# A two-layer attention and RWKV-7 backbone: two plain pairs and no GpSimd in the MLPs, low-rank weights in halves

## The chip, the cores and the metric

The kernel runs on one core of one Trainium2 chip. The metric is the device time of one execution in microseconds; the lower the better. The engines are named as the profile names them: PE is TensorE, DVE is VectorE, ACT is ScalarE, POOL is GpSimd, and SP issues the DMAs.

## What is computed

A trunk of 256 context tokens and 512 latent tokens of width 1024 passes two layers. Layer 0 is windowed attention and an MLP over all 768 tokens, layer 1 is RWKV-7 time mixing in both directions and an MLP over the 512 latent tokens alone. Everything is float32.

```python
def sq_relu_mlp(h, w1, w2):
    return jnp.square(jax.nn.relu(h @ w1)) @ w2          # D_FF = 4 * 1024
...
def rwkv_features(h, mu, w_rkv, w0, w1, w2, a0, a1, a2, k_k, k_a):
    xr, xw, xk, xv, xa, xg = [h + xx * mu[m] for m in range(6)]
    r = heads(xr @ w_rkv[0])
    k = heads(xk @ w_rkv[1])
    v = heads(xv @ w_rkv[2])
    decay = tuple(
        heads(jnp.exp(-jnp.exp(-jax.nn.softplus(-(w0[d] + jnp.tanh(xw @ w1[d]) @ w2[d]).astype(F32)) - 0.5)))
        for d in range(2))
    a = heads(jax.nn.sigmoid((a0 + (xa @ a1) @ a2).astype(F32)))
...
    def gate(d):
        return (jax.nn.sigmoid(xg @ g1[d]) @ g2[d]).astype(F32)
```

## The kernel before

Features lie on the 128 partitions, tokens along the free axis; 1024 features are 8 blocks, called `f` or `k`. A float32 product is made of three matmuls (`mm3`, L366, L368 and L370): each operand is split into a high part, a rounded copy (mostly on ACT), and a low part, the remainder (a subtraction, on DVE or POOL); high by high, high by low and low by high are added up in PSUM.

**The MLPs** (`mlp`). The hidden width 4096 is 32 tiles `m` of 128 columns of W1. Tiles are taken in pairs. One pair is plain: `first_pair` (matmuls at L762) runs 8 feature blocks x 3 x 2 token halves x 2 tiles, 96 matmuls. Fifteen pairs go through `pair`, a scheme of Winograd's kind with 7 half-size products in place of 8: 7 x 4 x 3 = 84 matmuls. A token half has H = 384 columns in the MLP of layer 0 (MLP0 below) and 256 in that of layer 1 (MLP1). The price of the seven products are sums on the side of the weights (`wsum`, L811 to L814, for each pair), sums on the side of the operand (`block_sums`, L698 to L718, once for each MLP, over 4 blocks `k` and 4 sums `b`, each split into `mbh` and `mbl`), and sums of the products (`add` into `keep` and `mrelu`, L799). The square of the ReLU is split into `hid` and multiplied by W2 (`w2`, L841 on) in 8 blocks; its result is added to the trunk X (L664, L860). POOL takes part: a11-a21 (L814), the low parts of products 1, 5 and 6 (L789), half of the operand's last two sums (L711, L713, L716) and in MLP0 each second low part of W2 (L852).

**The features** of layer 1 come from products with full weights (r, k, v) and from low-rank maps: `low` makes the 64 or 128 inner columns, `lora2` and `gate` the second product, one block `f` at a time. A decay block (`decay`, L1145) is a product (L1099), a sigmoid on ACT into `sg` (L1154) whose 12 boundary columns POOL sets to zero (L1152), a scan on DVE into `cs` (L1159, L1161) and a store. The second maps' weights come through `side_weights` (L1028): one 128x1024 matrix in two transfers of 512 columns (L1036), each split on ACT (L338) or POOL (L340) in turn and on DVE (L341). Each matrix is asked for when its first block begins (`if f == 0`).

**What sets the order.** A scheduler with a model of the engines' times lays out one queue for each engine before the run; each engine then works through its own in order, and an instruction that waits holds all behind it. SP's queue of DMAs is one of them. Tiles come from rings of a fixed number of buffers, so a new tile waits until the last user of the old one is done.

```python
with self.behind_norm():
    self.block_sums(u2, H, bh, bl)
...
(eng or nc.vector).tensor_tensor(wl, raw, wh.bitcast(F32), ALU.subtract)
...
nc.gpsimd.memset(sg[:, :, 64 * d:64 * d + 1], 0.0)
```

Of the kernel before, what the change touches and what calls it, by code (L numbers as in the profile page):

```python
# [9 lines left out]
F32 = mybir.dt.float32  # L10
# [164 lines left out]
class K:  # L175
# [522 lines left out]
    def block_sums(self, u2, H, bh, bl):  # L698
# [8 lines left out]
        for b, i in ((4, 0), (3, 1), (5, 2), (6, 3)):  # L707
            for k in range(4):
                t = ts[k][i]
                if b == 5:  # L710
                    nc.gpsimd.tensor_tensor(t, ts[k][0], t, ALU.subtract)  # L711
                if b == 6:
                    nc.gpsimd.tensor_tensor(t, t, ts[k][0], ALU.subtract)  # L713
                act = nc.scalar.activation(bh[:, b, k], t, AF.Copy)
                eng = nc.gpsimd if b == 6 else nc.vector
                lo = eng.tensor_tensor(bl[:, b, k], t, bh[:, b, k].bitcast(F32), ALU.subtract)  # L716
                if b == 5:
                    self.sums_ins = (act.ins, lo.ins)  # L718

    def mlp(self, l, bc):  # L720
# [15 lines left out]
        self.normed_w(u2, Xk, bc, g2, self.ada[:, u0 + 3], l, n, bh, bl)  # L736
        parts = self.halves if l == 0 else lambda ps: [(ps[:, 0:S], slice(0, S))]
# [12 lines left out]
        def first_pair():  # L750
            banks, ws = [self.big("w1_ps") for _ in range(2)], []
            for j in range(2):
                raw = mp.tile([P, 1024], F32, tag="w1raw", bufs=NRW[l], name="w1raw")
                nc.sync.dma_start(raw, a["w1"][l, j])
                ws.append([self.wp.tile([P, 1024], F32R, tag=t, name=t) for t in ("whi", "wlo")])
                self.split(raw, *ws[j], eng=1)
            for k in range(NF):
                q = ((0, 6), (1, 2))[k // 4]
                for ps, (wh, wl) in zip(banks, ws):
                    for w, t, e in ((wh, bh, 0), (wh, bl, 1), (wl, bh, 2)):  # L760
                        for h in range(2):
                            nc.tensor.matmul(ps[:, 512 * h:512 * h + H], w[:, k * P:k * P + P], t[:, q[h], k % 4],  # L762
                                             start=(k == 0 and e == 0), stop=(k == NF - 1 and e == 2))
            with self.behind_norm():
                self.block_sums(u2, H, bh, bl)
            hid = hid_pair()
            for j, ps in enumerate(banks):
# [3 lines left out]
                nc.scalar.activation(hid[0][:, j], r, AF.Square)  # L771
                nc.vector.tensor_tensor(r, r, r, ALU.mult)
                nc.vector.tensor_tensor(hid[1][:, j], r, hid[0][:, j].bitcast(F32), ALU.subtract)
            return hid

        def pair(m, hid, j):
# [8 lines left out]
            def product(tag, raw, b, eng=None):  # L785
# [3 lines left out]
                (eng or nc.vector).tensor_tensor(wl, raw, wh.bitcast(F32), ALU.subtract)  # L789
# [16 lines left out]
            def square(i):  # L806
                nc.vector.scalar_tensor_tensor(c[i], c[i], 0.0, c[i], ALU.max, ALU.mult)  # L807
                nc.scalar.activation(hid[0][:, j + i], c[i], AF.Copy)
                nc.vector.tensor_tensor(hid[1][:, j + i], c[i], hid[0][:, j + i].bitcast(F32), ALU.subtract)  # L809

# [6 lines left out]
            add(c11, product("t", a12, 1, nc.gpsimd), p1)  # L817
# [13 lines left out]

        def w1(g):
            hid = first_pair() if g == 0 else hid_pair()
            for j in range(0, GF, 2):
                if g or j:
                    with self.behind_norm() if GF * g + j == 2 else ExitStack():
                        pair(GF * g + j, hid, j)
            hids[g] = hid

        def w2(g):  # L840
# [3 lines left out]
            for m in range(8):  # L844
# [119 lines left out]
    def rwkv_features(self, xs, scan):  # L964
# [131 lines left out]
        def lora2(parts, w, x, f):  # L1096
            for i in range(2):
                for o, sl in parts:
                    nc.tensor.matmul(o, w[i][:, f * P:f * P + P], x[:, sl], start=(i == 0), stop=(i == 1))  # L1099

        def low(w, m):
# [3 lines left out]
            for k in range(NF):  # L1105
# [881 lines left out]
```

## Time and profile before

| | |
|---|---|
| runs | 2232.52, 2230.0 and 2235.05 us, median 2232.52 |
| profiled execution | 2226.51 us, span of the trace 2224.5 us |
| mean granted TensorE clock | 0.939 |
| TensorE (PE) busy | 1999.1 us, 90% of the span |
| VectorE (DVE) | 1597.0 us, 72% |
| ScalarE (ACT) | 992.5 us, 45% |
| GpSimd (POOL) | 441.1 us, 20% |

In the trace MLP0's first matmul is at 464.19 us and its stage ends near 986; the features follow until about 1320, the scans and the readout until about 1848, and MLP1 from 1855.70 to the end. Times in the trace are from the start of the span. A row of the timeline has the start, the duration, the engine, the line, the operation, its output and inputs, and in brackets how long the engine was idle before it and what ended that. A merged row ("x6") has the duration of the whole. Neighbouring instructions of an engine overlap a little, so the distance of two starts is shorter than one duration. Granted clock 1.00 is the 2.4 GHz level, and about half of it in a stretch means the 1.2 GHz level.

### The profile page before, as it was taken

The numbers are of one execution on the slowest core, as the hardware profiler recorded it, in microseconds if no ns is written. First come the engines' busy times: TensorE is split into PE (matmuls) and PEld (weight loads), VectorE is DVE, ScalarE is ACT, GpSimd is POOL, SyncE is SP. The second block draws the span as 40 slices with busy tenths as digits, with TensorE's granted clock in tenths as the row PEclk, the third lists the DMA queues.
The fourth block names the chain that finished last, engine by engine and source line by source line (L and its number), as shares of the span: only waits on it lengthen the run. The fifth ranks groups of instructions, "written<-read, shape, count | busy, mean of one in ns | idle before, by whom it ended". The sixth has DMA issues, their size and how long they took to land. (4 is left out here: it accounts for less than half of the span.)

```text
span 2224.5 us, 42844 instructions
## 1 busy us (share of the span) xinstructions
PE 1999.1 (90%) x16616; PEld 1690.3 (76%) x16616; DVE 1597.0 (72%) x3263; ACT 992.5 (45%) x2026; POOL 441.1 (20%) x470
## 2 busy tenths in 40 slices
PE   5999999979999999988979797698759887999999
PEld 4876766868999999976856686586648656899897
DVE  4465565378777777679687575988898658988774
ACT  4355454253223322336554446567747445334331
POOL 0123232034222232210111101000000103323220
PEclk8999999979999999988989898798879897999999
DMA  8345461112222122134255344113211312333322
GB/s 292 106 123 155 133 221 59 57 52 74 72 65 71 63 72 65 53 119 167 86 188 220 117 138 154 52 33 106 87 54 50 133 49 72 109 100 100 104 82 81
DMA packets 125115, 229.81 MB, mean 103 GB/s; under 512 B 13937, under 2 KB 48497, under 8 KB 124529
## 3 DMA queue, kind: packets, MB, share of 16 engines
q1 hardware_dynamic: 124912, 227.08, 31.3%
q8 instruction: 131, 2.15, 0.4%
q14 instruction: 72, 0.58, 0.1%
HBM read 191.80 MB, written 32.60 MB: 101 GB/s over the span
## 5 line engine op out<-in xcount | busy, mean ns | idle before, releaser
L366 PE MATMUL w_ps<-hid,w2h 128*128 128x512 f32 (+1 forms) x768 | 231.1, 356 | 0.3
L368 PE MATMUL w_ps<-hid,w2h 128*128 128x512 f32 (+1 forms) x768 | 230.7, 354 | 0.4 <-DVE hid L809 0.4
L370 PE MATMUL w_ps<-hid,w2l 128*128 128x512 f32 (+1 forms) x768 | 230.6, 354 | 0.0
L850 ACT ACTIVATE w2h<-w2raw 128x256 fp32r<-128x256 f32 (+1 forms) x192 | 92.9, 487 | 287.0 <-PE w_ps L368 259.7
L664 DVE SCALAR_TENSOR_TENSOR X<-w_ps,ada,X 128x256 f32<-128x256 f32 (+1 forms) x256 | 145.2, 610 | 101.0 <-PE w_ps L370 100.6
L366 PE MATMUL w1p_ps<-mbh,whi 128*128 128x384 f32 x420 | 142.4, 341 | 6.2 <-ACT whi L788 4.8
L370 PE MATMUL w1p_ps<-mbh,wlo 128*128 128x384 f32 x420 | 142.8, 341 | 4.4 <-DVE wlo L789 3.0
L366 PEld LDWEIGHTS w_ps<-hid,w2h 128*128 128x128 f32 x768 | 129.6, 188 | 18.1 <-DVE X L860 1.1
L368 PE MATMUL w1p_ps<-mbl,whi 128*128 128x384 f32 x420 | 142.4, 339 | 0.0
L368 PEld LDWEIGHTS w_ps<-hid,w2h 128*128 128x128 f32 x768 | 126.1, 188 | 20.9 <-DVE hid L809 0.6
L370 PEld LDWEIGHTS w_ps<-hid,w2l 128*128 128x128 f32 x768 | 125.9, 188 | 20.8
L366 PE MATMUL w1p_ps<-mbh,swh 128*128 128x256 f32 x420 | 120.7, 288 | 15.5 <-ACT swh L788 9.4
L368 PE MATMUL w1p_ps<-mbl,swh 128*128 128x256 f32 x420 | 119.9, 286 | 0.3 <-DVE mbl L716 0.3
L370 PE MATMUL w1p_ps<-mbh,swl 128*128 128x256 f32 x420 | 118.7, 285 | 0.0
L789 POOL TENSOR_TENSOR swl<-w1raw,swh 128x512 fp32r<-128x512 f32 x45 | 69.9, 1556 | 197.1 <-ACT swh L788 115.4
L568 DVE CUSTOM_DVE_ANT_0 sm<-sc_ps,consts,vecs 128x256 f32<-128x256 f32 (+2 forms) x96 | 71.5, 760 | 38.4 <-PE sc_ps L566 17.9
L1447 PE MATMUL g_ps<-pad,bk 128*128 128x128 f32 x640 | 95.8, 300 | 3.3 <-ACT pad L1444 1.7
L366 PEld LDWEIGHTS w1p_ps<-mbh,swh 128*128 128x128 f32 x420 | 81.4, 194 | 19.0 <-ACT swh L788 9.6
L1447 PEld LDWEIGHTS g_ps<-pad,bk 128*128 128x128 f32 x640 | 83.4, 205 | 13.4 <-ACT pad L1444 7.2
L852 POOL TENSOR_TENSOR w2l<-w2raw,w2h 128x256 fp32r<-128x256 f32 x64 | 58.1, 908 | 178.8 <-ACT w2h L850 178.8
L341 DVE TENSOR_TENSOR wlo<-wraw,whi 128x1024 fp32r<-128x1024 f32 (+1 forms) x57 | 55.1, 983 | 52.7 <-ACT whi L338 32.9
L583 POOL TENSOR_SCALAR sm<-sm,sums 128x256 f32<-128x256 f32 (+2 forms) x96 | 63.6, 681 | 128.7 <-DVE sums L581 57.9
(424 smaller groups left out, 5629.5 us busy)
## 6 DMA issues: line engine op xcount, KB each, us to landing
ada_w<-ada_w SPq DMA_DIRECT2D x160, 256.0 KB, 3.5
w1raw<-w SPq DMA_DIRECT2D x64, 512.0 KB, 3.3
w2raw<-w SPq DMA_DIRECT2D x128, 128.0 KB, 2.1
w2raw<-w SPq DMA_DIRECT2D x64, 256.0 KB, 2.7
kt<-ada_w SPq DMA_DIRECT2D x32, 256.0 KB, 5.1
feat<-cs SPq DMA_DIRECT2D x16, 390.0 KB, 2.4
cs<-feat SPq DMA_DIRECT2D x24, 260.0 KB, 2.8
wraw<-wq SPq DMA_DIRECT2D x8, 512.0 KB, 3.8
```

The source lines that it names most:

```text
L341: nc.vector.tensor_tensor(lo, raw, hi.bitcast(F32), ALU.subtract)
L366: nc.tensor.matmul(o, wh, cut(xh, sl), start=start, stop=False)
L368: nc.tensor.matmul(o, wh, cut(xl, sl), start=False, stop=False)
L370: nc.tensor.matmul(o, wl, cut(xh, sl), start=False, stop=stop)
L568: nc.vector.tensor_tensor_reduce(sm[:, :nk], ps[:, :nk], self.c["band"][:, b0:b0 + nk], rs[:, h:h + 1], self.v["sink"][:, hd:hd + 1], ALU. ...
L583: nc.gpsimd.tensor_scalar(sms[h][:, :nk], sms[h][:, :nk], sums[:, h:h + 1], 1.0, ALU.mult, ALU.mult)
L664: self.nc.vector.scalar_tensor_tensor(self.X[:, m, sl], ps[:, sl], self.ada[:, u, m, s:s + 1], self.X[:, m, sl], ALU.mult, ALU.add)
L789: (eng or nc.vector).tensor_tensor(wl, raw, wh.bitcast(F32), ALU.subtract)
L850: nc.scalar.activation(wh, raw, AF.Copy)
L852: eng.tensor_tensor(wl, raw, wh.bitcast(F32), ALU.subtract)
L1447: nc.tensor.matmul(g[:, P * k:P * k + P], it.BK[:, d, b + k], pv[:, :, k], start=True, stop=True)
```

## The change

- In both MLPs two pairs are plain, tiles 0, 1 and tiles 2, 3 (`plain_weights`, `plain_pair`), and fourteen go through `pair`. The weights of tile 2 lie in the ring of W2's tiles. The operand's block sums are made while the second plain pair runs; the last four go into tiles of the `keep` ring and are split behind that pair.
- In the MLPs all that POOL did is done on DVE. The first pair's square is made in the way of the others (`square`).
- `side_weights` gives halves of 128x512 from a ring of two for each of the high and the low part. The first half of a matrix is asked for in block 5 of the one before it, the second half in block 1 of its own use.

```diff
-        for b, i in ((4, 0), (3, 1), (5, 2), (6, 3)):
+        for b, i in ((4, 0), (3, 1), (5, 2)):
             for k in range(4):
                 t = ts[k][i]
                 if b == 5:
-                    nc.gpsimd.tensor_tensor(t, ts[k][0], t, ALU.subtract)
...
+                    nc.vector.tensor_tensor(t, ts[k][0], t, ALU.subtract)
+                self.sums_ins = self.block_split(b, k, t, bh, bl)
+        for k in range(4):
+            nc.vector.tensor_tensor(t4[k], ts[k][3], ts[k][0], ALU.subtract)
+
+    def block_split(self, b, k, t, bh, bl):
+        act = self.nc.scalar.activation(bh[:, b, k], t, AF.Copy)
+        lo = self.nc.vector.tensor_tensor(bl[:, b, k], t, bh[:, b, k].bitcast(F32), ALU.subtract)
+        return act.ins, lo.ins
...
+        def plain_weights(m, own):
+
+            raw = mp.tile([P, 1024], F32, tag="w1raw", bufs=NRW[l], name="w1raw")
+            nc.sync.dma_start(raw, a["w1"][l, m])
+            w = 1024 if own else P * GF
+            ws = []
+            for c in range(0, 1024, w):
+                if own:
+                    ws.append([self.wp.tile([P, w], F32R, tag=t, name=t) for t in ("whi", "wlo")])
+                else:
+                    ws.append([mp.tile([P, w], F32R, tag=t, bufs=5, name=t) for t in ("w2h", "w2l")])
+                self.split(raw[:, c:c + w], *ws[-1], eng=1)
+            return [(h[:, c:c + P], l_[:, c:c + P]) for h, l_ in ws for c in range(0, w, P)]
+
+        def plain_pair(ws, turns):
+
+            banks = [self.big("w1_ps") for _ in range(2)]
+            for i, k in [(i, k) for k in range(NF) for i in range(2)] if turns else itertools.product(range(2), range(NF)):
                 q = ((0, 6), (1, 2))[k // 4]
...
+        def square(c, hid, j):
+            nc.vector.scalar_tensor_tensor(c, c, 0.0, c, ALU.max, ALU.mult)
+            nc.scalar.activation(hid[0][:, j], c, AF.Copy)
+            nc.vector.tensor_tensor(hid[1][:, j], c, hid[0][:, j].bitcast(F32), ALU.subtract)
...
-                (eng or nc.vector).tensor_tensor(wl, raw, wh.bitcast(F32), ALU.subtract)
+                nc.vector.tensor_tensor(wl, raw, wh.bitcast(F32), ALU.subtract)
...
-            nc.gpsimd.tensor_tensor(a21, a11, a21, ALU.subtract)
+            nc.vector.tensor_tensor(a21, a11, a21, ALU.subtract)
...
         def w1(g):
-            hid = first_pair() if g == 0 else hid_pair()
+            if g == 0:
+                rs = plain_pair([plain_weights(0, True), plain_weights(1, True)], True)
+                with self.behind_norm():
+                    ws.extend([plain_weights(2, False), plain_weights(3, True)])
+                    self.block_sums(u2, t4, H, bh, bl)
+            hid = hid_pair()
...
+                elif m == 2:
+                    rs = plain_pair(ws, False)
+                    for i in range(2):
+                        square(rs[i], hid, j + i)
+                    for k in range(4):
+                        self.sums_ins = self.block_split(6, k, t4[k], bh, bl)
...
-                    eng = nc.gpsimd if l == 0 and m % 2 else nc.vector
-                    eng.tensor_tensor(wl, raw, wh.bitcast(F32), ALU.subtract)
+                    nc.vector.tensor_tensor(wl, raw, wh.bitcast(F32), ALU.subtract)
...
         def side_weights(src):
...
+            halves = {}
+
+            def part(f):
+
+                i = f // 4
+                if i not in halves:
+                    halves[i] = [rp.tile([P, 512], F32R, tag=t, bufs=2, name=t) for t in ("swh", "swl")]
+                    raw = tmp(512, "swr")
+                    nc.sync.dma_start(raw, src[:, 512 * i:512 * i + 512])
+                    self.split(raw, *halves[i])
+                return [t[:, f % 4 * P:f % 4 * P + P] for t in halves[i]]
+
+            part(0)
+            return part
...
         def decay(d, f):
-            if f == 0:
-                w2[d] = side_weights(a["lw2"][d])
+            if f == 1:
+                w2[d](4)
+            elif f == 5:
+                w2[d + 1] = side_weights(a["la2"] if d else a["lw2"][1])
```

`low`, `keys` and `gate` are changed in the manner of `decay`.

The order of two queues shows what moved. First DVE at the start of MLP1, before: the operand's block sums are split at L716 (`mbl<-nu,mbh`), the weight sums are made at L811 to L813 and split at L789 (`swl`), a product is added at L799.

```order
2495 L812 TENSOR_TENSOR wsum<-wsum,w1raw 128x512
2496 L716 TENSOR_TENSOR mbl<-nu,mbh 128x256 x6
2497 L813 TENSOR_TENSOR wsum<-w1raw,wsum 128x512
2498 L716 TENSOR_TENSOR mbl<-nu,mbh 128x256 x2
2499 L799 TENSOR_TENSOR mrelu<-w1p_ps,keep 128x256
2500 L716 TENSOR_TENSOR mbl<-nu,mbh 128x256 x2
2501 L789 TENSOR_TENSOR swl<-wsum,swh 128x512 x3
```

And DVE at the same place in the changed kernel (L718 splits the operand's sums, L819 to L822 make the weight sums, L802 splits them, L785 and L787 are the square and its remainder `hid`, L875 is the low part of W2):

```order
2616 L718 TENSOR_TENSOR mbl<-keep,mbh 128x256
2617 L820 TENSOR_TENSOR wsum<-wsum,w1raw 128x512
2618 L822 TENSOR_TENSOR w1raw<-w1raw 128x512
2619 L718 TENSOR_TENSOR mbl<-keep,mbh 128x256 x3
2620 L875 TENSOR_TENSOR w2l<-w2raw,w2h 128x512 x2
2621 L787 TENSOR_TENSOR hid_19564<-mrelu,hid_19563 128x512 x2
2622 L821 TENSOR_TENSOR wsum<-w1raw,wsum 128x512
2623 L787 TENSOR_TENSOR hid_19564<-mrelu,hid_19563 128x512
2624 L812 TENSOR_TENSOR mrelu<-w1p_ps,keep 128x256
2625 L785 SCALAR_TENSOR_TENSOR mrelu<-mrelu 128x512
2626 L875 TENSOR_TENSOR w2l<-w2raw,w2h 128x512
2627 L802 TENSOR_TENSOR swl<-wsum,swh 128x512 x3
```

The split of the weight sums has moved behind all block sums, behind the first low parts of W2 and behind the hidden tiles of the second plain pair; a11-a21 (L822) has come into the queue from POOL.

Second, POOL among the decays, before (`swh<-swr` splits a half of a low-rank matrix, `whi<-wraw` weights of r and k):

```order
158 L1152 MEMSET sg 128x12
159 L340 TENSOR_SCALAR swh<-swr 128x512
160 L340 TENSOR_SCALAR whi<-wraw 128x1024
161 L1152 MEMSET sg 128x12
162 L340 TENSOR_SCALAR whi<-wraw_11127 128x512
163 L1152 MEMSET sg 128x12 x5
164 L340 TENSOR_SCALAR whi<-wraw_11340 128x512
165 L1152 MEMSET sg 128x12 x2
166 L340 TENSOR_SCALAR swh<-swr 128x512
167 L1152 MEMSET sg 128x12 x7
```

And in the changed kernel:

```order
52 L1188 MEMSET sg 128x12 x2
53 L340 TENSOR_SCALAR whi<-wraw 128x1024
54 L340 TENSOR_SCALAR swh<-swr 128x512
55 L1188 MEMSET sg 128x12 x2
56 L340 TENSOR_SCALAR whi<-wraw_11129 128x512
57 L1188 MEMSET sg 128x12 x2
58 L340 TENSOR_SCALAR swh<-swr 128x512
59 L340 TENSOR_SCALAR whi<-wraw 128x1024
60 L1188 MEMSET sg 128x12 x3
61 L340 TENSOR_SCALAR whi<-wraw_11340 128x512
62 L1188 MEMSET sg 128x12 x7
```

The split for the second direction stood behind nine memsets and ahead of seven; it now stands behind six and ahead of ten.

## Rows read from the trace of the kernel before

**Rows 1.** Windows (bounds, length, busy us and count by engine, PEclk, DMA): MLP0, features.
```profile
484.00:500.00 16.00, 8.92 (x32) 7.77 (x32) 13.24 (x15) 8.59 (x19) 16.00 (x11) 0.70 0.09 33
500.00:510.00 10.00, 8.36 (x45) 7.50 (x44) 9.84 (x10) 4.90 (x9) 10.00 (x8) 0.97 0.09 28
510.00:520.00 10.00, 8.11 (x46) 7.11 (x44) 9.97 (x12) 2.09 (x4) 5.44 (x4) 1.00 0.30 92
...
600.00:700.00 100.00, 100.00 (x577) 93.32 (x576) 74.11 (x123) 29.47 (x57) 28.76 (x26) 1.00 0.21 69
...
1100.00:1150.00 50.00, 39.36 (x188) 29.57 (x187) 40.28 (x39) 26.64 (x46) 8.92 (x18) 0.90 0.45 163
```

**Rows 2.** Windows of MLP1; order of the columns PE, PEld, DVE, ACT, POOL, as above.
```profile
1873.70:1883.00 9.30, 0.00 (x0) 0.00 (x0) 9.30 (x13) 3.31 (x10) 8.15 (x10) 0.63 0.00 0
1883.00:1887.00 4.00, 3.88 (x19) 3.77 (x20) 3.84 (x8) 4.00 (x10) 2.30 (x2) 0.59 0.42 135
...
1892.00:1897.00 5.00, 0.67 (x3) 0.67 (x4) 5.00 (x8) 2.15 (x5) 0.98 (x1) 0.61 0.38 126
1897.00:1902.00 5.00, 5.00 (x23) 4.45 (x23) 5.00 (x10) 1.21 (x3) 2.16 (x1) 0.70 0.26 88
1902.00:1907.00 5.00, 5.00 (x44) 5.00 (x43) 5.00 (x7) 2.40 (x5) 4.33 (x3) 1.00 0.27 103
...
2000.00:2100.00 100.00, 99.95 (x639) 90.84 (x638) 77.75 (x121) 39.50 (x68) 28.46 (x20) 1.00 0.30 98
```

**Rows 3.** Timeline of TensorE at the start of MLP0.
```profile
482.12 0.51 PE L762 MATMUL w_ps<-mbl,whi 128*128 128x384 f32 x2
...
483.51 0.34 PE L366 MATMUL w1p_ps<-mbh,whi 128*128 128x384 f32 x1
...
485.94 0.44 PE L370 MATMUL w1p_ps<-mbh,wlo 128*128 128x384 f32 x1 [1.45 <-DVE wlo L789]
...
492.74 0.69 PE L366 MATMUL w1p_ps<-mbh,whi 128*128 128x384 f32 x1 [4.77 <-ACT whi L788]
```

**Rows 4.** Timeline of TensorE at the start of MLP1.
```profile
1883.12 0.58 PE L366 MATMUL w1p_ps<-mbh,swh 128*128 128x256 f32 x1 [9.43 <-ACT swh L788]
...
1896.33 0.58 PE L366 MATMUL w1p_ps<-mbh,swh 128*128 128x256 f32 x1 [4.57 <-DVE keep L799]
```

**Rows 5.** Timeline of DVE at the start of MLP1.
```profile
1876.02 5.25 DVE L716 TENSOR_TENSOR mbl<-nu,mbh 128x256 fp32r<-128x256 f32 x6
...
1882.33 0.75 DVE L716 TENSOR_TENSOR mbl<-nu,mbh 128x256 fp32r<-128x256 f32 x2
```

**Rows 6.** Groups of L789 by form: durations in ns (min/median/max), first and last start.
```profile
L789 POOL TENSOR_TENSOR wlo<-w1raw,whi x45: 1283/1300/2009, 493.0 to 942.6; 128x512 fp32r<-128x512 f32 x45
L789 DVE TENSOR_TENSOR wlo<-wsum,whi x45: 673/681/1494, 494.9 to 930.1; 128x512 fp32r<-128x512 f32 x45
...
L789 DVE TENSOR_TENSOR wlo<-w1raw,whi x15: 678/1368/1767, 485.2 to 917.9; 128x512 fp32r<-128x512 f32 x15
```

**Rows 7.** The page's costliest groups: MLP0's update of X (busy, mean ns, idle).
```profile
L664 DVE SCALAR_TENSOR_TENSOR X<-w_ps,ada,X 128x256 f32<-128x256 f32 (+1 forms) x256 | 145.2, 610 | 101.0 <-PE w_ps L370 100.6
```

**Rows 8.** Timeline of all engines at the second direction's decays.
```profile
1124.86 0.86 SPq L1036 DMA_DIRECT2D swr<-lw  x2
...
1128.54 2.84 POOL L340 TENSOR_SCALAR swh<-swr 128x512 fp32r<-128x512 f32 x1 [5.19 <-DMA swr<-lw]
...
1131.43 0.80 PE L1099 MATMUL wl_ps<-tw,swh 128*128 128x512 f32 x1 [6.95 <-POOL sg L1152]
...
1134.54 11.91 DVE L1161 TENSOR_TENSOR_SCAN cs<-pm,sg 128x780 f32<-128x780 f32 x7 [1.42 <-ACT sg L1154]
...
1142.20 0.50 PE L366 MATMUL r_ps<-mxh,whi 128*128 128x512 f32 x1 [0.70 <-ACT sg L1154]
```

**Rows 9.** Timeline of TensorE at the gate.
```profile
1260.45 0.80 PE L366 MATMUL g_ps<-tw,swh 128*128 128x512 f32 x1 [4.29 <-ACT gt L1253]
```

**Rows 10.** Timeline of TensorE in the scan stage.
```profile
1658.04 2.19 PE L1522 MATMUL mg<-mt,gm 32*32 32x32 f32 x74 [19.37 <-DVE mt L1512]
```

More of the change, by code (lines that the diff above doesn't have):

```diff
@@ L736, in mlp @@
         self.normed_w(u2, Xk, bc, g2, self.ada[:, u0 + 3], l, n, bh, bl)
+        t4 = [mp.tile([P, H], F32, tag="keep", bufs=4, name="keep") for _ in range(4)]
         parts = self.halves if l == 0 else lambda ps: [(ps[:, 0:S], slice(0, S))]
@@ L748, in block @@
             return [w[:, 512 * h:512 * h + 512] for w in turn["w"]]
[L750 to L757, printed above, removed]
-                q = ((0, 6), (1, 2))[k // 4]
[L759 to L767, printed above, removed]
+        def plain_weights(m, own):
[10 more added lines that the diff above has]
+            return [(h[:, c:c + P], l_[:, c:c + P]) for h, l_ in ws for c in range(0, w, P)]
@@ new lines, in plain_pair @@
+        def plain_pair(ws, turns):
+            banks = [self.big("w1_ps") for _ in range(2)]
+            for i, k in [(i, k) for k in range(NF) for i in range(2)] if turns else itertools.product(range(2), range(NF)):
+                q = ((0, 6), (1, 2))[k // 4]
+                wh, wl = ws[i][k]
+                for w, t, e in ((wh, bh, 0), (wh, bl, 1), (wl, bh, 2)):
+                    for h in range(2):
+                        nc.tensor.matmul(banks[i][:, 512 * h:512 * h + H], w, t[:, q[h], k % 4],
+                                         start=(k == 0 and e == 0), stop=(k == NF - 1 and e == 2))
+            rs = []
+            for ps in banks:
@@ L822, in pair @@
             add(c12, p3, w)
-            square(0)
-            z = add(keep(), product("t", a21, 5, nc.gpsimd), q)
+            square(c[0], hid, j)
+            z = add(keep(), product("t", a21, 5), q)
             add(c22, p5, z)
-            add(c21, product("o", a22, 6, nc.gpsimd), z)
-            square(1)
+            add(c21, product("o", a22, 6), z)
+            square(c[1], hid, j + 1)
         def hid_pair():
             return [mp.tile([P, GF, n], F32R, tag=f"hid{i}", bufs=2, name=f"hid{i}") for i in range(2)]
+        ws = []
         def w1(g):
-            hid = first_pair() if g == 0 else hid_pair()
-            for j in range(0, GF, 2):
-                if g or j:
-                    with self.behind_norm() if GF * g + j == 2 else ExitStack():
-                        pair(GF * g + j, hid, j)
+            if g == 0:
[4 more added lines that the diff above has]
+            hid = hid_pair()
+            for j in range(0, GF, 2):
+                m = GF * g + j
+                if m == 0:
+                    for i in range(2):
+                        square(rs[i], hid, i)
+                elif m == 2:
+                    rs = plain_pair(ws, False)
+                    for i in range(2):
+                        square(rs[i], hid, j + i)
+                    for k in range(4):
+                        self.sums_ins = self.block_split(6, k, t4[k], bh, bl)
+                else:
+                    pair(m, hid, j)
             hids[g] = hid
@@ L1120, in low_decay @@
             th = tmp(T, "th")
-            for o, sl in (yield from low(w_lo, 1)):
+            for o, sl in (yield from low(w_lo, 1, lambda: w2.update(la1=side_weights(a["la1"])))):
                 nc.scalar.activation(th[:, sl], o, AF.Tanh)
@@ L1133, in low_rate @@
         def low_rate():
-            for o, sl in (yield from low(side_weights(a["la1"]), 4)):
+            for o, sl in (yield from low(w2["la1"], 4, lambda: w2.update({0: side_weights(a["lw2"][0])}))):
                 nc.scalar.activation(AH[0:64, sl], o[0:64], AF.Copy)
```

58 lines of the change are left out of this document (23 added, 35 removed).

## The prediction

> **What bounds the kernel now.** I read the windows first, then the timeline of TensorE around each window in which it is not full, then the groups by form for prices. In the middle of the MLPs TensorE is the bound: full at clock 1.00 for 100 us, with DVE at 74.11 and POOL at 28.76 beside it [rows 1]; MLP1 has the same, 99.95 with DVE at 77.75 [rows 2]. What the change does to DVE there is free as long as DVE stays under TensorE's pace. The time lies at three starts. In 484 to 500 TensorE does 32 matmuls at clock 0.70 [rows 1]. In 1873.7 to 1883 it does nothing, in 1892 to 1897 three matmuls, and then 23 where the next 5 us hold 44 [rows 2]. Among the features, 1100 to 1150 holds 50.00-39.36 = 10.64 us of idle TensorE [rows 1].
>
> The reader should see in the MLP starts a busy DVE beside an idle TensorE: 9.30 of 9.30 us [rows 2]. TensorE names DVE wlo and ACT whi in MLP0 [rows 3], ACT swh and DVE keep in MLP1 [rows 4]; these come late because the weight sums that they split stand in DVE's queue among the operand's block sums, and because both are stretched: six 128x256 remainders take 5.25 us, 0.87 each, while two a little later take 0.75, a pitch of 0.33 for a duration of 0.41 [rows 5].
>
> **Part 1, the second plain pair.** It adds 96-84 = 12 matmuls to each MLP. In MLP0 eight of this form take 483.51-482.12 = 1.39 us [rows 3], 0.174 each: +2.1 us. In MLP1 44 take 5.00 us [rows 2], 0.114 each: +1.4 us. Against this stands cover. A plain pair needs neither block sums nor weight sums: 96 x 0.174 = 16.7 us of TensorE in MLP0 and 96 x 0.114 = 10.9 in MLP1, in which DVE makes the sums.
>
> MLP0: 32 matmuls at 0.174 are 5.6 us, so 484 to 500 loses 10.4, of which 1.45 and 4.77 are the two waits [rows 3] and the rest is half clock and small gaps; the next two stretches idle 1.64 and 1.89 [rows 1]. Together 13.9; less 2.1, it can bring 11.8 at most. I walked DVE's new queue with the short prices (0.33, 0.47 and 0.60 us for 256, 384 and 512 columns; the first is a row's pitch [rows 5], the others are estimates from it and from the 673 of a 512 [rows 6], in proportion). The second pair's weights are split by about 486.5, a gap that the two products standing ahead in TensorE's queue fill; the last sum is split at about 501, when TensorE has just ended the second pair, and w2 of the first pair follows. I take **-11**, ends -12 and -4 (one wait comes back, with its half clock, 7).
>
> MLP1, lost by the same count: 9.3, 5.00 - 3 x 0.114 = 4.7, 5.00 - 23 x 0.114 = 2.4, and 4.00 - 19 x 0.114 = 1.8 [rows 2], together 18.2; less 1.4, 16.8 at most. But here the cover is short. TensorE has 10.9 us behind 1873.7, to about 1884.6. DVE has in that time 16 plain remainders, four L711 and four L714 at 0.33, the second pair's 1024 columns, three squares, four weight sums and two w2l, which by the short prices ends with two remainders of hid at about 1887. So w2 waits some 2.4 us, a keep in the pair behind it perhaps 1, and the clock may fall once more, as it did for 2.4 in 1897 to 1902. 16.8 less 5.8 is 11, and 13.4 if the clock holds. I take **-13**, ends -17 and -6.
>
> **Part 2, no POOL in the MLPs.** Per pair four 128x512 operations go to DVE, and in MLP0 four w2l of 256 columns. POOL takes 1283 ns at least for a wlo, DVE 673 for the same form [rows 6]. The cost at the starts is in the walks above. In the steady part, 45 POOL wlo from 493.0 to 942.6, three in a pair [rows 6], put a pair at some 31 us; DVE gets 4 x 0.60 + 4 x 0.33 = 3.7 us, 12% of it. What DVE has now is 74% [rows 1], but part of that is stretch: wlo<-w1raw has the form of wlo<-wsum and a median of 1368 against 681, though its minimum is 678 [rows 6]. By short prices DVE's own work in a pair is three sums and four remainders at 0.60, seven adds at 0.47, four steps of the square at 0.87, four w2l at 0.33 and 16 updates of X at about 0.5 (mean 610, with its other form, [rows 7]): some 20.5 us, 66%; with the addition 78%. With the stretch kept it is 74 + 12 = 86%. Both stay under TensorE's 100, so I take **0**: the 3.7 us are hidden behind TensorE, and without that cover they would cost 3.7 in each of 14 pairs.
>
> The Trainium skill ("SBUF — State Buffer", section "Who interferes with whom") says that a DVE instruction with two SBUF inputs and a POOL instruction that reads SBUF exclude each other, each for the whole of the other's time. By that rule the stretch goes with POOL and the 78% would hold, with the sum as it is; the doubled median agrees.
>
> **Part 3, the halves.** The chain at the second decay is plain: SP asks for swr<-lw at 1124.86, POOL stands with the split until 1128.54+2.84 = 1131.38, the memsets of sg queued behind it come only then, and TensorE waits 6.95 us for one [rows 8]. Then the eight decays run as fast as DVE's scans, seven in 11.91 us, until r_ps starts at 1142.20 [rows 8]. In the new order the second matrix is asked for and split within the first direction. Undone: 6.95, and 1 to 2 of what follows, as less stands behind the scans at the end. At the gate the first product behind a wait waits 4.29 [rows 9] for ACT's gt; with the halves split earlier the gate starts a v block sooner, and I count 3 of it. That is 11.5, and I take **-10**, because the 14 transfers and splits stay what they are and each now stands amid decays, where a split that waits for its DMA (up to 3.68 us, from SP's issue to POOL's start, [rows 8]) holds the sg behind it. Ends -15 and -2.
>
> **Part 4, what moves along.** The order of the scan stage changes a little too. TensorE has a wait of 19.37 us for DVE there [rows 10], so a reordering can give or take some. No row says which way: 0, ends -5 and +10.
>
> **Sum.** -11 - 13 + 0 - 10 + 0 = -34 against the profiled 2226.51. The median of the runs is 2232.52, 6.0 above; 2232.5 - 34 = **2198.5**.
>
> **Rivals.**
> A, the feature waits only move: the halves queue on SP, which is in order, behind the stores of cs, and the sg behind the splits. For it: the swr of before were issued late, not slow to land [rows 8]. Against it: in POOL's new queue two memsets or more stand between a split and the next. Gain 2 instead of 10: 2206.5. Chance 0.17.
>
> B, the second pair does not cover the sums: DVE is full through all of 1873.7 to 1907 [rows 2], and a sum that is late holds the products behind it. Then -6 in MLP1 and -8 in MLP0: 2208.5. Chance 0.13.
>
> C, DVE becomes the bound (the slower side). Place: every pair of both MLPs; remainders, sums, adds, squares and w2l share one queue in order. Price: where a wait of s us is left in each of 28 pairs, 28 s; the change turns slower where s passes 34/28 = 1.2. What decides is whether DVE's work in a pair passes TensorE's 31 us, or comes late in bursts. For it: MLP1 has 77.75 already [rows 2], and if 1368 [rows 6] is what such an operation costs with POOL silent too, four more make 74 + 18 + 4 = 96% and each burst is late. Against it: 678 and 681. With s = 1.7, +48: 2246. Chance 0.06.
>
> D, the scan stage loses one more wait like [rows 10], +19: 2217.5. Chance 0.07.
>
> E, more than forecast: both starts whole, -12 and -17, the features -15, the scan -3: 2185.5. Chance 0.10.
>
> The forecast itself: 0.47.
>
> **How the numbers follow.** The range runs from E to just above D, 2185 to 2220, and leaves out C, half of E and D together with A or B, some 0.17. A difference of 0.2%, 4.5 us, is about what a measurement of this kernel can tell from none. Faster by more than that: all but C and the joint upper tail, 0.88. Within it 0.05, slower 0.07.
>
> **What would show it.** Right: no wait of TensorE above 3 us in either MLP start; wlo<-w1raw on DVE at a median near 681; DVE at 76 to 80 in a full 100 us of MLP0 with TensorE at 100; no wait of TensorE for a POOL sg above 2 us, and r_ps some 8 us nearer to the start of the features. Wrong: TensorE under 98 in the steady part with DVE named (C), a wait of some 6 us for sg at another decay (A), w2 of MLP1 waiting over 6 us for hid (B), a longer way from the features to MLP1 (D).

## The result and the profile after

The changed kernel takes 2198.33 us, median of 4 runs (2191.91 to 2204.5), against 2231.26 (2229.87 to 2235.05) before: ratio 0.9849, 95% interval 0.9818 to 0.9881, 33 us faster. Forecast were 2198.5. The total came out; where it came from did not, as the experiments show. Two of the medians below, 2227.49 for the halves only and 2199.89 for gbc behind, count slow runs of 2331 and 4718 us and of 6409 us; without these they are 2226.09 and 2198.34.

The profiled execution takes 2196.83 us, span 2195.0, mean clock 0.943. PE is busy 1988.8 us (91%), DVE 1601.3 (73%), ACT 991.9 (45%), POOL 169.9 (8%, before 20%).

The windows that answer to [rows 1], start of MLP0 and its middle (length, then PE, PEld, DVE, ACT, POOL busy with counts, clock, DMA):

```profile
489.00:505.00 16.00, 16.00 (x94) 16.00 (x93) 16.00 (x30) 10.37 (x20) 0.00 (x0) 1.00 0.12 37
505.00:515.00 10.00, 10.00 (x59) 9.45 (x58) 9.71 (x18) 5.48 (x11) 0.00 (x0) 1.00 0.32 105
...
600.00:700.00 100.00, 100.00 (x576) 93.23 (x575) 80.17 (x148) 30.45 (x58) 0.00 (x0) 1.00 0.22 69
```

TensorE is full at once behind the first pair, at clock 1.00, where it did 32 matmuls in 16 us. In the middle nothing has changed for it: 576 matmuls in 100 us against 577, with DVE at 80.17 in place of 74.11.

What answers to [rows 2] and [rows 4], windows of MLP1 and the only waits of TensorE that the trace names between its first pair and the end:

```profile
1871.00:1876.00 5.00, 4.65 (x39) 4.33 (x37) 5.00 (x12) 4.13 (x9) 0.00 (x0) 1.00 0.00 0
1876.00:1881.00 5.00, 4.15 (x19) 3.45 (x20) 5.00 (x10) 3.45 (x7) 0.00 (x0) 1.00 0.62 210
```

```profile
1876.85 0.50 PE L368 MATMUL w_ps<-hid,w2h 128*128 128x512 f32 x1 [1.19 <-DVE hid L787]
1888.35 0.39 PE L366 MATMUL w1p_ps<-mbh,swh 128*128 128x256 f32 x1 [0.20 <-DVE keep L812]
```

The waits of 9.43 and 4.57 are gone; the one for hid that was expected at 2.4 is 1.19, and the clock doesn't fall. The whole of MLP1, before and after:

```profile
1855.70:2224.50 368.80, 347.55 (x2124) 312.60 (x2124) 286.49 (x438) 141.68 (x250) 101.24 (x72) 0.97 0.29 94
```

```profile
1846.60:2195.00 348.40, 342.13 (x2136) 309.46 (x2136) 275.53 (x494) 141.10 (x246) 0.00 (x0) 0.99 0.31 97
```

DVE does 56 instructions more in 11 us less, so its rows before were stretched. The groups by form that answer to [rows 6] say it outright (min/median/max in ns):

```profile
L802 DVE TENSOR_TENSOR wlo<-w1raw,whi x56: 678/683/692, 498.8 to 928.4; 128x512 fp32r<-128x512 f32 x56
```

In the features the wait of 6.95 for sg [rows 8] is gone and the one of 4.29 for gt [rows 9] is 0.51; in their place stand one for the remainder of a half (`swl`) and longer ones for `mxl`, the low part of the mixed input that k is made from:

```profile
1025.72 1.01 PE L368 MATMUL k_ps<-mxl,whi 128*128 128x512 f32 x2 [3.22 <-DVE mxl L1102]
...
1128.36 0.79 PE L1128 MATMUL wl_ps<-tw,swl 128*128 128x512 f32 x1 [1.73 <-DVE swl L341]
...
1133.53 0.76 PE L366 MATMUL r_ps<-mxh,whi 128*128 128x512 f32 x1 [0.58 <-ACT sg L1190]
...
1245.77 0.50 PE L366 MATMUL g_ps<-tw,swh 128*128 128x512 f32 x1 [0.51 <-ACT gt L1294]
```

So 6.95 + 4.29 = 11.2 us of waits went down to 0.5, but over all the features TensorE's idle time fell by 3.1 us only (363.43 - 320.53 = 42.9 before, 357.65 - 317.87 = 39.8 after). Its waits for mxl in the products of k went from 0.9 to 5.1 us together. `r_ps`, the first product behind the decays, starts 154.7 us behind the last update of X in MLP0 where it was 156.0: 1.3 us nearer, and 8 were forecast as a sign of being right.

Stage lengths tell more than totals here. Each number below is worked out from starts in one profiled execution: of MLP0's first matmul, of its last update of X, of the last gt, of MLP1's first matmul, and the end of the span. In the kernel before the last gt starts at 1349.66, so the features end there and not near 1320 as said above.

| kernel | to MLP0 | MLP0 | features | scan | MLP1 |
|---|---|---|---|---|---|
| before | 464.2 | 522.0 | 363.5 | 506.0 | 368.8 |
| changed | 469.1 | 509.7 | 357.7 | 510.1 | 348.4 |
| changed, again | 464.8 | 509.9 | 358.3 | 513.4 | 348.5 |
| halves only | 472.7 | 522.1 | 361.0 | 510.0 | 366.5 |
| both MLP parts | 463.9 | 510.6 | 362.2 | 504.6 | 349.4 |
| both MLP parts, again | 469.1 | 510.0 | 361.7 | 507.5 | 349.2 |
| no POOL only | 468.8 | 514.6 | 361.3 | 505.6 | 356.0 |
| plain pair only | 469.7 | 517.0 | 363.7 | 506.7 | 361.2 |
| low part twice | 474.6 | 511.0 | 354.9 | 513.6 | 353.3 |
| gate as before | 466.8 | 510.7 | 362.1 | 507.7 | 349.2 |
| decays as before | 467.8 | 509.8 | 358.1 | 513.9 | 349.3 |
| gbc behind | 470.3 | 510.4 | 355.8 | 514.7 | 348.5 |
| lanes first | 469.1 | 510.2 | 356.5 | 502.0 | 349.4 |

The first column is the attention, whose code no kernel here touches: 464 to 475, with 4.3 and 5.2 us between two executions of one kernel. A good part of what single totals differ by lies there; in the two kernels that were profiled twice the other columns repeat within 0.6 us in the MLPs and the features and within 3.3 us in the scan.

### The profile page after: what moved, and what is told of

Same layout as the page of the kernel before. It is cut to its first block, busy times and chain, and to the rows that moved or that the text cites. A ratio compares the mean times of both kernels' runs of the same rounds, so it can differ in the third digit from the quotient of the medians.

```text
span 2195.0 us, 42674 instructions
## 1 busy us (share of the span) xinstructions
PE 1988.8 (91%) x16640; PEld 1687.8 (77%) x16640; DVE 1601.3 (73%) x3443; ACT 991.9 (45%) x2022; POOL 169.9 (8%) x262
## 5 line engine op out<-in xcount | busy, mean ns | idle before, releaser
L664 DVE SCALAR_TENSOR_TENSOR X<-w_ps,ada,X 128x256 f32<-128x256 f32 (+1 forms) x256 | 145.8, 611 | 74.3 <-PE w_ps L370 73.8
L366 PEld LDWEIGHTS w_ps<-hid,w2h 128*128 128x128 f32 x768 | 130.6, 188 | 16.7 <-ACT w2h L874 0.7
L368 PE MATMUL w1p_ps<-mbl,whi 128*128 128x384 f32 x392 | 131.9, 337 | 0.0
L370 PE MATMUL w1p_ps<-mbh,wlo 128*128 128x384 f32 x392 | 131.6, 337 | 0.0
L366 PE MATMUL w1p_ps<-mbh,whi 128*128 128x384 f32 x392 | 131.1, 337 | 0.0
L368 PE MATMUL w1p_ps<-mbl,swh 128*128 128x256 f32 x392 | 110.4, 283 | 0.0
L366 PE MATMUL w1p_ps<-mbh,swh 128*128 128x256 f32 x392 | 110.0, 283 | 0.2 <-DVE keep L812 0.2
L370 PE MATMUL w1p_ps<-mbh,swl 128*128 128x256 f32 x392 | 109.5, 283 | 0.0
L568 DVE CUSTOM_DVE_ANT_0 sm<-sc_ps,consts,vecs 128x256 f32<-128x256 f32 (+2 forms) x96 | 71.6, 760 | 38.8 <-PE sc_ps L566 18.2
L875 DVE TENSOR_TENSOR w2l<-w2raw,w2h 128x256 fp32r<-128x256 f32 (+1 forms) x192 | 96.3, 503 | 0.1
L883 DVE SCALAR_TENSOR_TENSOR X<-w_ps,ada,X 128x512 f32<-128x512 f32 x64 | 47.8, 747 | 50.0 <-PE w_ps L370 49.9
L366 PEld LDWEIGHTS w1p_ps<-mbh,swh 128*128 128x128 f32 x392 | 74.7, 191 | 2.3 <-DVE keep L812 0.6
L1632 PE MATMUL x_ps<-z,gm 128*64 128x64 f32 x768 | 70.2, 240 | 6.7 <-issue 2.6
```

The costliest lines, as they stand in the source:

```text
L366: nc.tensor.matmul(o, wh, cut(xh, sl), start=start, stop=False)
L368: nc.tensor.matmul(o, wh, cut(xl, sl), start=False, stop=False)
L370: nc.tensor.matmul(o, wl, cut(xh, sl), start=False, stop=stop)
L568: nc.vector.tensor_tensor_reduce(sm[:, :nk], ps[:, :nk], self.c["band"][:, b0:b0 + nk], rs[:, h:h + 1], self.v["sink"][:, hd:hd + 1], ALU. ...
L664: self.nc.vector.scalar_tensor_tensor(self.X[:, m, sl], ps[:, sl], self.ada[:, u, m, s:s + 1], self.X[:, m, sl], ALU.mult, ALU.add)
L875: nc.vector.tensor_tensor(wl, raw, wh.bitcast(F32), ALU.subtract)
```

## The experiments

**Theory**: the second pair's cover makes the starts (parts 1 and 3 carry the gain, part 2 nothing). **Rivals**: the stretch that POOL puts on DVE makes them; DVE becomes the bound; the halves only move waits. The first four kernels take the change apart; all ran with the kernel before at 2230.74 us.

### Part 3 alone

Edit: of the change's diff the hunks of side_weights, low, decay, keys and gate.

> The kernel before with part 3 alone (the low-rank weights in halves, asked for ahead). Theory (parts add up): the MLP stages keep their lengths, 522 us for MLP0 (first matmul to last update of X) and 368.8 us for MLP1; the way from the last X of MLP0 to the last gt is shorter by 4 to 8 us, as it was by 5.8 in the changed kernel (363.5 to 357.7); no wait of TensorE for a POOL sg above 2 us. In all 4 to 8 us faster, a ratio of 0.9965 to 0.998. Rival (the waits only move): the features keep their 363 us and the ratio lies between 0.999 and 1.002.

Measured: 2227.49 us, ratio 0.9983 (0.997 to 0.9997). MLP0 is as before, MLP1 at 366.5; the features are 2.5 us shorter, the scan 4.0 longer. TensorE doesn't wait for POOL's sg any more, and for gt 0.8 us. So the edit does what it says, but most of the 11.2 us is given back: in the features, where TensorE's waits for mxl in k come to 5.6 us, and in the scan, whose code it doesn't touch. The total falls between theory and rival.

### Parts 1 and 2 alone

Edit: the other hunks, those of the MLPs.

> The kernel before with parts 1 and 2 alone (second plain pair, no POOL in the MLPs), the features as before. Theory (parts add up): MLP0 12 us and MLP1 20 us shorter, as in the trace of the changed kernel, the rest as before, a ratio of about 0.986 (31 us). Rival (the halves are what the total needs): the ratio is above 0.99. A second rival (the halves cost what they bring, through the scan's order): the ratio is that of the whole change, 0.985, or better.

Measured: 2197.58 us, ratio 0.9863 (0.9843 to 0.9882). MLP0 510.6, MLP1 349.4, the rest as before: the second rival holds as much as the theory, since this is the whole change's time within the intervals.

### Part 2 alone

```diff
-                    nc.gpsimd.tensor_tensor(t, ts[k][0], t, ALU.subtract)
+                    nc.vector.tensor_tensor(t, ts[k][0], t, ALU.subtract)
...
-                eng = nc.gpsimd if b == 6 else nc.vector
+                eng = nc.vector
...
-            add(c11, product("t", a12, 1, nc.gpsimd), p1)
+            add(c11, product("t", a12, 1), p1)
```

and so for the rest of POOL's work in the MLPs; one plain pair stays.

> The kernel before with part 2 alone: in both MLPs all of POOL's work goes to DVE, one plain pair as before. Theory (the cover decides): the stretch of DVE's rows goes (median of wlo<-w1raw near 681 ns), but all block sums stand in one queue ahead of the weight sums and nothing runs over them: TensorE still loses 8 to 12 of the 14 us at the start of MLP0 and 12 to 18 of the 20 at the start of MLP1; 4 to 12 us faster, ratio 0.995 to 0.998. Rival (the stretch was the cause): the starts lose less than 5 us each, and the ratio is below 0.99. Rival (DVE becomes the bound): a ratio above 1.002, TensorE under 98% in the middle of an MLP.

Measured: 2207.30 us, ratio 0.989 (0.9874 to 0.9907). MLP0 is 7.4 us shorter, MLP1 12.8. The theory falls: with all of the sums in one queue and nothing over them, DVE gets through far earlier all the same. The rival holds by the total; that each start loses less than 5 us doesn't come out at MLP1, where one wait alone is 6.01. TensorE's waits at the two starts, and the group of the low parts:

```profile
491.01 0.44 PE L366 MATMUL w1p_ps<-mbh,whi 128*128 128x384 f32 x1 [2.94 <-ACT whi L788]
...
1873.16 0.58 PE L366 MATMUL w1p_ps<-mbh,swh 128*128 128x256 f32 x1 [6.01 <-ACT swh L788]
```

```profile
L789 DVE TENSOR_TENSOR wlo<-w1raw,whi x60: 680/686/705, 491.3 to 940.9; 128x512 fp32r<-128x512 f32 x60
```

The waits of 4.77 and 9.43 [rows 3, 4] became 2.94 and 6.01, that of 4.57 for keep went altogether, and four operations more per pair cost nothing that shows. The group's maximum is 705 ns where it was 1767 [rows 6], and 717 over all low parts of products.

At the start of MLP1 the stretch can be read on the path itself. The wait of 9.43 is for ACT's swh, and that waits for the sum of L813. DVE from the first of the four L705 to L813, before and with part 2 alone:

```profile
1870.50 3.60 DVE L705 TENSOR_TENSOR nu<-nu 128x256 f32<-128x256 f32 x4
...
1881.20 1.20 DVE L813 TENSOR_TENSOR wsum<-w1raw,wsum 128x512 f32<-128x512 f32 x1
```

```profile
1863.83 1.42 DVE L705 TENSOR_TENSOR nu<-nu 128x256 f32<-128x256 f32 x4
...
1871.73 0.69 DVE L813 TENSOR_TENSOR wsum<-w1raw,wsum 128x512 f32<-128x512 f32 x1
```

Without a pause in either, DVE takes 10.70 us for twelve instructions before, and 7.90 for 22 with POOL's among them. That is 2.8 of the 3.4 us by which the wait shrank. How much the rest of part 2 owes to POOL's own pace (1300 ns for a low part that DVE makes in 686), no run separates.

### Part 1 alone

The kernel of parts 1 and 2 with POOL's share restored:

```diff
-            nc.vector.tensor_tensor(t4[k], ts[k][3], ts[k][0], ALU.subtract)
+            nc.gpsimd.tensor_tensor(t4[k], ts[k][3], ts[k][0], ALU.subtract)
...
-            nc.vector.tensor_tensor(a21, a11, a21, ALU.subtract)
+            nc.gpsimd.tensor_tensor(a21, a11, a21, ALU.subtract)
...
```

and so for the low parts that POOL made.

> The kernel before with part 1 alone: a second plain pair in both MLPs, while POOL keeps its share (a11-a21, low parts of products 1, 5, 6, the operand's last two sums, each second low part of W2 in MLP0). Theory (the cover decides): the stretch stays (median of a 512-column wlo<-w1raw on DVE above 1000 ns), yet most of the gain is there: MLP0 8 to 12 us and MLP1 10 to 18 us shorter, ratio 0.987 to 0.992. Rival (the stretch was the cause): POOL's long instructions still hold DVE through the second pair, each start keeps half of its loss, ratio 0.993 or more.

Measured: 2219.26 us, ratio 0.9951 (0.9934 to 0.9967), MLP0 5.0 us shorter, MLP1 7.6: the rival's figure. The cover runs out because DVE and POOL hold each other up under it. TensorE behind the second pair, then POOL and DVE in that time:

```profile
507.89 0.62 PE L366 MATMUL w_ps<-hid,w2h 128*128 128x512 f32 x2 [1.84 <-ACT w2h L874]
...
514.47 1.01 PE L370 MATMUL w_ps<-hid,w2l 128*128 128x512 f32 x2 [4.85 <-DVE w2l L875]
```

```profile
487.84 7.74 POOL L711 TENSOR_TENSOR nu<-nu 128x384 f32<-128x384 f32 x1 [46.57 <-DVE nu L705]
...
496.52 1.33 POOL L711 TENSOR_TENSOR nu<-nu 128x384 f32<-128x384 f32 x1
```

```profile
498.19 1.50 DVE L802 TENSOR_TENSOR wlo<-w1raw,whi 128x512 fp32r<-128x512 f32 x1
499.62 3.95 DVE L718 TENSOR_TENSOR mbl<-nu,mbh 128x384 fp32r<-128x384 f32 x3
```

The same POOL subtraction takes 7.74 us and 1.33; on DVE a 512 takes 1.50 in place of 0.68, and three 384 remainders 3.95, 1.3 each, where the short pitch is 0.47. These durations fit an instruction that waits for whole instructions of the other engine. The Trainium skill ("SBUF — State Buffer", section "Who interferes with whom") describes just that for a DVE instruction with two SBUF inputs against a POOL instruction that reads SBUF. The runs agree: with no POOL work in the MLPs no low part of a product takes above 717 ns.

Parts 1 and 2 add up: in MLP0 5.0 + 7.4 = 12.4 against 11.4 and 12.0 for both, in MLP1 7.6 + 12.8 = 20.4 against 19.4 and 19.6. Of the 33 us part 2 is worth 20 (by the two stages) to 23 (by the total, 2230.74 - 2207.30), part 1 10 to 13, and part 3 next to nothing beside them.

### How much room DVE has

The changed kernel, with

```diff
-                nc.vector.tensor_tensor(wl, raw, wh.bitcast(F32), ALU.subtract)
+                for _ in range(2):
+                    nc.vector.tensor_tensor(wl, raw, wh.bitcast(F32), ALU.subtract)
```

> The changed kernel, with the DVE subtraction that makes a product's low weights issued twice (the same result written again): 7 x 0.60 = 4.2 us more DVE work in each of 28 pairs, DVE at about 91 to 93% of a pair in place of 78. Theory (TensorE is the bound of the steady part, the starts are bound by DVE): TensorE stays above 98% in a full 100 us of MLP0, and the loss comes at the two starts alone, 2 to 8 us in all, ratio to the kernel before 0.985 to 0.990. Rival (DVE's bursts come late long before it is full): TensorE below 97% in the middle of MLP0, 15 us or more lost, ratio above 0.992.

Measured, against 2230.83 us before, as for the next three: 2201.16, ratio 0.987 (0.9849 to 0.9891).

```profile
600.00:700.00 100.00, 100.00 (x576) 93.60 (x575) 94.61 (x174) 29.02 (x57) 0.00 (x0) 1.00 0.22 69
```

TensorE stays at 100.00 with DVE at 94.61, so the steady part had room for all of it; in 2000 to 2100, in MLP1, it is 100.00 with DVE at 97.59. What is lost lies mostly in MLP1, 353.3 against 348.4. DVE as the bound (C) is out, even at this load.

### Which half of part 3 brings what

The changed kernel with the gates' matrices asked for in block 0 again (the request for the first of them in `keys` is dropped):

```diff
-            if f == 1:
-                g2[d](4)
-            elif f == 5 and d == 0:
-                g2[1] = side_weights(a["lg2"][1])
+            if f == 0:
+                g2[d] = side_weights(a["lg2"][d])
+                g2[d](4)
```

> The changed kernel, with the gates' matrices asked for as before (both halves in block 0 of their use), the decays and la2 with halves ahead. In this kernel's order of TensorE the gbc of the next to last readout stands behind the last merge again. Theory (the halves bring some 5 us in the features, and a gbc that has come ahead of the merge in TensorE's queue loses 4 to 5 in the scan): scan stage 505 to 507 us in place of 510; the wait of 4.29 at the gate may come back; ratio 0.983 to 0.985. Rival (the scan's loss is not from the gbc): scan stage 509 us or more.

Measured: 2203.21 us, ratio 0.9875 (0.9852 to 0.9898). The features lose 4.4 us (362.1), and TensorE's wait for gt is 4.4 long again: this part of the forecast was right. The scan is 507.7, near the theory's 505 to 507, but the ratio missed. This kernel still has the decays' matrices in halves, and no wait for POOL's sg; without any halves, in both MLP parts alone, that wait is 6.96 and 6.97, and the features are as long, 362.2 and 361.7. So the wait that the halves take away at the decays brings nothing in the sum. TensorE waits longer for mxl in k, earlier in the stage, 5.6 us against 2.1 and 1.0; that the halves, whose splits DVE now makes there too, cause this is not shown.

The same edit for the decays (in decay, `f == 0` asks for lw2[d] and both halves; la2 in front of keys):

```diff
-            if f == 1:
-                w2[d](4)
-            elif f == 5:
-                w2[d + 1] = side_weights(a["la2"] if d else a["lw2"][1])
+            if f == 0:
+                w2[d] = side_weights(a["lw2"][d])
+                w2[d](4)
```

> The changed kernel, with the decays' and the rate's second matrices asked for as before (both halves in block 0 of their use), the gates with halves ahead. Theory: the wait for POOL's sg behind a split comes back, 4 to 7 us, with its half clock; the gate keeps its earlier start; features 2 to 5 us longer than the changed kernel's 357.7, scan stage 505 to 507 us (the gbc stands behind the merge), ratio 0.984 to 0.987. Rival (the gain in the features is the gates' alone): features 359 us or less.

Measured: 2199.17 us, ratio 0.9851 (0.9833 to 0.987), features 358.1, scan 513.9. No wait for POOL's sg came back; the longest in the decays is 3.34, for ACT's sg. So the rival holds: the features' gain is the gates'. Asked for in block 0, the second direction's matrix comes in time here:

```profile
1114.61 1.96 POOL L340 TENSOR_SCALAR swh<-swr 128x512 fp32r<-128x512 f32 x1 [5.91 <-DMA swr<-lw]
...
1116.63 0.50 PE L1128 MATMUL wl_ps<-tw,swh 128*128 128x512 f32 x1 [0.63 <-POOL swh L340]
```

POOL splits while TensorE still has products of k, and TensorE waits 0.63. The wait of 6.87 to 6.97 stands in all four kernels that have no halves; in this order of the queues it stays away though the decays ask as before. And the scan is long here too, with gbc behind the merge, which speaks against the cause that I had for it.

### What takes it back in the scan

In the scan stage DVE works through lane steps (`lane`, `ltmp`), transposes the lanes (`mt`, `dt`), and TensorE merges them (`mg`); there are six such rounds. A readout behind a round takes a square root on ACT, its reciprocal on DVE (`grs`), splits it (`grh`), and spreads it with a matmul (`gbc`). In the changed kernel TensorE meets a gbc of a readout ahead of the last merge:

```profile
1720.76 0.76 PE L1736 MATMUL gbc<-grh,s_gbsel 64*128 64x512 f32 x1 [5.51 <-DVE grh L396]
1722.71 3.62 PE L1563 MATMUL mg<-mt,gm 32*32 32x32 f32 x128 [1.19 <-DVE mt L1553]
```

First edit, gbc behind the merge:

```diff
-                    nc.tensor.matmul(bc, gbsel[0:64, 2 * d + fl], held["r"], start=True, stop=True)
+                    with tc.issue_after(its[5].mg) if it.n == 4 else ExitStack():
+                        nc.tensor.matmul(bc, gbsel[0:64, 2 * d + fl], held["r"], start=True, stop=True)
```

(`it.mg` is the merge's last matmul.)

> The changed kernel with one edit: the gbc matmuls of the next to last readout are issued behind the last merge's matmuls, as in the kernel before. Theory (gbc stood ahead of the merge and held it while it waited for DVE's grh): TensorE's wait of 5.5 us for grh goes, the scan stage falls from 510 to 505 to 507 us, all else stays, ratio 0.982 to 0.984, the fastest of all. Rival (the merge waits for DVE's lanes anyway): the scan stage stays at 509 to 511 us, ratio 0.985.

Measured: 2199.89 us, ratio 0.986 (0.9844 to 0.9876), scan 514.7. The rival holds, with a longer scan than it said:

```profile
1722.74 3.63 PE L1563 MATMUL mg<-mt,gm 32*32 32x32 f32 x128 [7.51 <-DVE mt L1553]
```

The merge starts at the same time and waits for DVE's transpose `mt` instead. So DVE's queue is where to look. In the changed kernel, between the last iteration's lane steps:

```profile
1712.70 0.69 DVE L341 TENSOR_TENSOR ow<-of,oh 128x512 fp32r<-128x512 f32 x1 [0.33 <-issue]
...
1713.50 0.68 DVE L341 TENSOR_TENSOR ow<-of,oh 128x512 fp32r<-128x512 f32 x1
...
1714.20 1.29 DVE L341 TENSOR_TENSOR ow<-of,oh 128x512 fp32r<-128x512 f32 x2
...
1717.14 1.75 DVE L1716 RECIPROCAL grs<-grs 64x256 f32<-64x256 f32 x1 [1.28 <-ACT grs L1715]
...
1720.64 2.02 DVE L1553 STREAM_TRANSPOSE mt<-lane 128x1024 f32<-128x1024 f32 x1
```

With the MLP parts alone the order is another, and the transpose comes straight behind the lanes:

```profile
1713.25 0.32 DVE L1530 TENSOR_TENSOR lane<-lane,ltmp 128x10 f32<-128x10 f32 x3
1713.61 2.05 DVE L1535 STREAM_TRANSPOSE mt<-lane 128x1024 f32<-128x1024 f32 x1
...
1719.48 2.50 DVE L341 TENSOR_TENSOR ow<-of,oh 128x512 fp32r<-128x512 f32 x4
```

Four splits of 0.60, the reciprocal's wait of 1.28, its 1.75 and two grh of some 0.4 make 6 to 7 us. From the start of the fifth merge to that of the sixth it takes 71.1 us in the kernel before and 78.9 in the changed one. Second edit:

```diff
-                self.split(t, oh[:, f], ol[:, f])
+                with tc.issue_after(its[5].back):
+                    self.split(t, oh[:, f], ol[:, f])
...
+                with tc.issue_after(its[5].back) if it.n == 4 else ExitStack():
+                    nc.scalar.activation(rs, vps[0:64, 0:256], AF.Sqrt, bias=geps[0:64])
+                    nc.vector.reciprocal(rs, rs)
+                    self.rows_hl(rs, 256, held["r"])
```

(`its[5].back` is the last merge's second transpose on DVE.)

> The changed kernel with an edit in the scan stage alone: the four splits of the saved readout (ow<-of,oh) and the reciprocal and grh of the next to last readout are issued behind the transposes of the last merge, where the kernel before has them. Theory (these 6 to 7 us of DVE work and wait, which the new order put among the last iteration's lanes, make the merge late, and so give back what the halves bring): from the fifth merge to the sixth 71 to 73 us in place of 78.9, scan stage 504 to 507 us, features as in the changed kernel, 355 to 358, a ratio of 0.981 to 0.983, 4 to 6 us faster than the changed kernel in the same batch. Rival (what is moved comes to stand in the tail behind and delays wo1 as much): scan stage 509 us or more, no difference.

> The changed kernel as it is, beside the two others on one chip. Theory: ratio 0.984 to 0.987; MLP0 510, MLP1 348 to 349, features 355 to 358, scan stage 509 to 511 us; what differs between its runs is the attention (464 to 473 us to MLP0's first matmul).

> Parts 1 and 2 alone, again. Theory (the halves bring nothing net): within 2 us of the changed kernel in the same batch, ratio 0.985 to 0.988, features 361 to 364 and scan stage 504 to 507 us. Rival (the halves bring their 5 us): 4 us or more slower than the changed kernel.

Measured in one batch, before at 2231.58 us: lanes first 2190.34, ratio 0.9812 (0.9788 to 0.9836); the change again 2197.64, 0.9846 (0.9829 to 0.9864); both MLP parts again 2199.41, 0.9857 (0.9836 to 0.9878).

```profile
1712.98 2.06 DVE L1553 STREAM_TRANSPOSE mt<-lane 128x1024 f32<-128x1024 f32 x1
1714.90 1.92 DVE L1556 STREAM_TRANSPOSE dt<-lane 128x1024 f32<-128x1024 f32 x1
1716.66 2.46 DVE L341 TENSOR_TENSOR ow<-of,oh 128x512 fp32r<-128x512 f32 x4
1719.03 1.73 DVE L1718 RECIPROCAL grs<-grs 64x256 f32<-64x256 f32 x1
```

The sixth merge starts at 1715.19 (fifth at 1643.74: 71.5 us), the scan takes 502.0, and the features keep their 356.5. The theory holds, with more gain than it forecast, and this kernel beats both: 41 us under before, 7 under the change, its slowest run (2194.0) under the fastest of the change (2195.27). The halves without that edit are worth 1.8 us, inside the intervals.

## Why the prediction was right, and where it was not

The sum was -34, the runs show -33. That this agrees so well is luck in part: MLP1 gave 7 us more than its term, the features 4 to 5 less than theirs, and the scan took 4 to 7. Point by point:

- **MLP0**, -11: near in size, 12.3 and 12.1, a little past the end of -12 and the "11.8 at most", which counted the loss from 484 to 520 alone. **The reason was half wrong.** The prediction put it on cover (16.7 us of TensorE, "in which DVE makes the sums"); part 1 alone brings 5.0, part 2 alone 7.4.
- **MLP1**, -13 with ends -17 and -6: it was 20.4 and 20.3, beyond the end. Two things were left out. The lost time was counted in four windows, 18.2; over the whole stage TensorE's idle time fell by 21.25 - 6.27 = 15.0 and its busy time by 5.4 although it does 12 matmuls more, so there were about 21.8 to get (15.0, 5.4 and 1.4). A part of it lay behind the start, in what I took for full: from the first group's updates of X to the end it is 277.9 us before and 275.8 after, with eight matmuls more. Then 3.8 were held back for new waits and a falling clock: 1.4 came, and the clock held.
- **Part 2, 0**: this is the step that failed. The prediction named the stretch among the reasons for the late sums, but put it into part 2 as something that "goes" and lowers DVE's share, and priced it there only where DVE isn't the bound. At MLP1's start DVE never pauses while TensorE waits for it (9.30 of 9.30 us, [rows 2]), and there the stretch is TensorE's time (10.70 us for twelve instructions against 7.90 for 22): part 2 alone brings 20 to 23 of the 33 us. The walk of the new queue did use the short prices, so the total was right, but it put their effect to the second pair.
- The steady part, 0: right in MLP0. DVE 80.17 against 78 forecast, not 86; rival C fell at 94.61 with TensorE still at 100.00.
- **The halves**, -10: the features gave 5.8 and 5.2, inside the ends, and 3.4 to 4.5 against both MLP parts alone. Of the two terms, 3 for the gate was 4.4. **The 8.5 for the wait behind POOL's split is a second step that failed**: the wait went, as forecast, but nothing came of it. Without it and with the gate as before the features take 362.1 us, with it 362.2 and 361.7, and r_ps came 1.3 us nearer, not 8. Rival A, that the waits only move, holds there in effect, but with longer waits for DVE's mxl and not by SP's queue or a later sg; the wait was priced as if nothing else would hold TensorE up.
- **The scan**, 0 with ends -5 and +10: +4.1 and +7.4. "No row says which way" was too quick: the new order of DVE's queue showed the four splits and the reciprocal ahead of the transpose, and the rows have a price for each. Rival D named the stage; its price of 19 was far too much.
- B didn't come: the second pair covers the sums once POOL is silent. It does come, in half, where POOL works on (the wait of 4.85).

What stays open: why the starts of the features and of the scan shift by a few us with each new order. The misplaced instructions explain the scan of the changed kernel (78.9 and 81.3 us from the fifth merge to the sixth), of halves only and of gbc behind (78.1 and 78.7), but not that of decays as before and low part twice: there the transposes stand ahead of the splits again and it takes 74.3 and 73.8, yet the whole stage takes 513.9 and 513.6. This wasn't tried further.

## What to carry to other kernels

Where two engines stretch each other, count the stretch at the place where one of them ends last, not over the mean: an engine that looks free can cost more than it does, and taking its work away can gain even where the other engine gets more to do. A wait that is taken away is worth its length only if nothing else holds the engine up behind it. Take a change of several parts apart before believing its reasons; here the total agreed to a microsecond with a wrong split. And when an order is remade, read the queue of the engine that ends the next stage's longest wait: seven misplaced instructions there ate most of what the edit had won.

## What was not expected of the hardware

With one plain pair more and POOL at work, POOL and DVE subtractions side by side took 1.3 to 1.5 us for 0.68 on DVE and once 7.74 us for 1.33 on POOL; with no POOL work in the MLPs, 60 subtractions of one form on DVE lay between 680 and 705 ns. The attention, the same code in all kernels, took between 464 and 475 us from run to run, about what one part of this change is worth.
